# Conditioning columns in the gates stage: partition sums moved one call behind the sums over k, with two buffers between them

## The chip, the cores and the metric

The kernel runs on one core of a Trainium2 chip. The metric is the device time of one execution in microseconds (us); a kernel's time is the median of several executions.

## What is computed

A trunk of two layers works on 1024 latent tokens and 256 context tokens of width 1024. Cut to what matters here, a layer is:

```python
shift, scale, gate = split(silu(c) @ w_ada[l] + b_ada[l], 3)          # for the latent tokens
shift_c, scale_c, gate_c = split(silu(c_ctx) @ w_ada[l] + b_ada[l], 3) # for the context tokens
h = rms(x) * (1 + scale) + shift
... three mixers on parts of h @ w_in[l], each giving a product y @ w_p ...
ga, gb, gc = split(sigmoid(g), 3)                                     # g: the last 3072 columns of h @ w_in[l]
merged = ga * (ya @ w_pa) + gb * (yb @ w_pb) + gc * (yc @ w_pc)
x = x + gate * (merged @ w_out[l])
```

The conditioning vectors shift, scale and gate are 3072 numbers for each of c and c_ctx. They are a product of a vector of 1024 numbers with a 1024 x 3072 matrix. The kernel keeps them as columns: number n stands in partition n mod 128 of column n div 128 of the tile `adac[l]` (24 columns, two variants v, for c and c_ctx).

## The kernel before

Each layer goes through attention, a Fourier stage, products of the mixers, the stage `gates` and the stage `out_phase`. Matrix products in 32-bit precision are made of three matmuls (`mm3`, lines 237 to 239): each operand is split into a rounded part and a remainder (ScalarE at L212 and VectorE at L213 for weights), and TensorE adds high times high, low times high and high times low.

**The gates stage** (`gates`, L671) builds `merged` in blocks of 128 output channels, j = 0 to 7. For every j and every group of 512 latent tokens there are three branches b. For each, TensorE makes a projection of 24 matmuls for the gate (some were made in earlier stages and are fetched back as `lt`), ScalarE takes its tanh (L734), and VectorE multiplies it with the branch's product (`add`, L681 and L684), which is fetched as `lp` or, for b = 1, made by 12 matmuls for each j into a tile shown as `pt` (`product`). GpSimd sums the branches (L685). In layer 0 the context tokens are a third group.

**The conditioning columns** that later stages need are made inside this stage, 256 of them at a time, by `ada_dve` (L177). Layer 0 has twelve such steps, four for its own gate and eight for the shift and scale of layer 1, each for both variants (nv = 2). Layer 1 has four, for one variant. A step has three parts:

- Two DMAs of 512 KB fetch 1024 rows x 256 columns of `w_ada` into two `araw` tiles (L183).
- VectorE takes the sums over k: for each variant eight instructions (L192 for k = 0, L196 for the rest), each of which multiplies a 128 x 256 piece by the scalar of its partition and adds it into `aacc`.
- TensorE sums over the partitions: four matmuls with a column of ones (two for nv = 1) into the PSUM tile `o` (L200); then two small instructions of VectorE add the bias and write `adac` (L202).

`finish`, which `ada_dve` returns, holds the second and third part. `sums` (L690) is called twice for each j, after the first and the fifth of its six branch additions (i = 0 and i = 4). A call runs `finish` of the step whose DMAs the last call issued, and then issues the DMAs of the next step. So step k (from 0) is loaded in call k + 1 and finished in call k + 2. There are 16 calls in the stage, so the last step of layer 0 is finished at j = 6, i = 0.

**What sets the order.** The tile framework is entered with `schedule_with_timeline_sim=True` (L1127). It writes each engine's instruction stream itself, before the run: an instruction is issued when a timeline that the framework keeps has its inputs ready, and among those that are ready the one that stands earlier in the program goes first. Each engine then works through its stream in that fixed order, and waits on the chip where an input is late. `tc.keep_in_program_order(ins)` (L194) pins one instruction behind the one that was traced last on its engine: here the first sum of variant 0. The sums of variant 1 are not pinned. PSUM tiles in the stage are `mm` (2 buffers, projections of the first group), `s` (3, of the second), `pt` (2) and `o` (1) (L98). All DMAs go through the SyncE queue (SP), in order.

`aacc` is one buffer for each nv, taken when `finish` begins, so the first sum of a step must wait until the matmuls of the step before have read it.

Of the kernel before, what the change touches and what calls it, by code (L numbers as in the profile page):

```python
# [11 lines left out]
F32 = mybir.dt.float32  # L12
# [54 lines left out]
def trunk_kernel(ctx: ExitStack, tc: tile.TileContext, a: dict, out: bass.AP):  # L67
# [17 lines left out]
    def bank(tag):  # L85
        tags = banks["tags"]
        tag = tag if tag in tags else "g"
        return banks["pool"].tile([128, 512], F32, tag, bufs=tags[tag])

    def ta(n=512):  # L90
        t = tp.tile([128, 512], F32, "ta", bufs=2)
        return t[:, :n]

    def tb(n=512):
        t = tp.tile([128, 512], F32, "tb", bufs=2)
        return t[:, :n]
# [80 lines left out]
    def ada_dve(l, jb, nv, pool):  # L177

        raws = []
        for half in range(2):  # L180
            raw = pool.tile([128, 4, 256], F32, "araw", bufs=2)
            src = a["w_ada"][l, half * 512:(half + 1) * 512, jb * 128:jb * 128 + 256]
            nc.sync.dma_start(raw, src.rearrange("(k p) c -> p k c", p=128))  # L183
            raws.append(raw)

        def finish():
            acc = pool.tile([128, nv, 256], F32, f"aacc{nv}")
            for k in range(8):
                for v in range(nv):
                    sc = scol[:, k, v:v + 1]  # L190
                    if k == 0:
                        ins = DVE.tensor_scalar(acc[:, v, :], raws[0][:, 0, :], sc, None, ALU.mult)  # L192
                        if v == 0:
                            tc.keep_in_program_order(ins)  # L194
                    else:
                        DVE.scalar_tensor_tensor(acc[:, v, :], raws[k // 4][:, k % 4, :], sc, acc[:, v, :], ALU.mult, ALU.add)  # L196
            pa = bank("o")
            for i in range(2):
                for v in range(nv):
                    PE.matmul(pa[:, 2 * i + v:2 * i + v + 1], acc[:, v, i * 128:(i + 1) * 128], ones[:, 0:1], start=True, stop=True)  # L200
            for i in range(2):
                DVE.tensor_scalar(adac[l][:, jb + i, 0:nv], pa[:, 2 * i:2 * i + nv], bada[l][:, jb + i:jb + i + 1], None, ALU.add)  # L202

        return finish
# [11 lines left out]
    def w_cm(l, c0):  # L216

        return granule(a["w_in"][l, :, c0:c0 + 128].rearrange("(k p) c -> p k c", p=128), [128, KC, 128])
# [17 lines left out]
    def mm3(o, lh, ll, rh, rl, start, stop):  # L236
        PE.matmul(o, lh, rh, start=start, stop=False)  # L237
        PE.matmul(o, lh, rl, start=False, stop=False)  # L238
        PE.matmul(o, ll, rh, start=False, stop=stop)  # L239

    def proj_cm(o, wg, h, n):

        for k in range(KC):
            mm3(o[:, :n], wg[0][:, k, :], wg[1][:, k, :], h[0][k], h[1][k], k == 0, k == KC - 1)
# [14 lines left out]
    def new_h(g):  # L259

        n = GROUPS[g][1]
        pool = bigs["C" if g == "C" else "L"]
        halves = [[pool.tile([128, KC // 2, n], F32R, f"h{x}{i}{g}") for i in range(2)] for x in "hl"]
        H[g] = [[halves[x][k // 4][:, k % 4, :] for k in range(KC)] for x in range(2)]
        return H[g]

    def split(hi, lo, src):
        ACT.copy(hi, src)  # L268
        DVE.tensor_tensor(lo, src, hi.bitcast(F32), ALU.subtract)  # L269
# [274 lines left out]
    def stored(S, key, n):  # L544
        S[key] = dp.tile([128, n], F32, "d" + "_".join(map(str, key)))
        return S[key]
# [6 lines left out]
    def fetched(st, src, n=512, bufs=4, tag="ld"):  # L553
        t = st.tile([128, 512], F32, tag, bufs=bufs)[:, :n]
        nc.sync.dma_start(t, src)
        return t
# [114 lines left out]
    def gates(l, groups, S, ada, side, yb):  # L671

        mp = Pool(tc, name="mp", bufs=1, side=side)
        zq = Pool(tc, name="zq", bufs=1, side=side)
        lat = [g for g in groups if g != "C"]
        hC = new_h("C") if "C" in groups else None
        todo = []

        def add(m, b, t, n, pp):
            if b == 0:  # L680
                DVE.scalar_tensor_tensor(m, t, 1.0, pp, ALU.add, ALU.mult)  # L681
            else:
                s = tb(n)
                DVE.scalar_tensor_tensor(s, t, 1.0, pp, ALU.add, ALU.mult)  # L684
                POOL.tensor_tensor(m, m, s, ALU.add)  # L685

        def branch(b, j, g):
            return fetched(mp, S["P", b, j, g], GROUPS[g][1], 3, f"lp{b}")

        def sums():  # L690
            if todo:
                todo.pop()()
            if ada:
                todo.append(ada_dve(*ada.pop(0), zq))

        def product(j, g):
            n = GROUPS[g][1]
            pp = bank("pt")
            for kb in range(2):
                c = (j % 2) * 128  # L700
                mm3(pp[:, :n], pg[0][:, kb, c:c + 128], pg[1][:, kb, c:c + 128],
                    yb[g][0][:, kb, :], yb[g][1][:, kb, :], kb == 0, kb == 1)
            return pp[:, :n]

        for j in range(8):
            M = {g: mp.tile([128, GROUPS[g][1]], F32, "m" + g, bufs=2) for g in groups}
            W = {}
            if j % 2 == 0:
                raw = zq.tile([128, 2, 256], F32, "praw")
                nc.sync.dma_start(raw, a["w_pb"][l, :, j * 128:j * 128 + 256].rearrange("(k p) c -> p k c", p=128))  # L710
                pg = [zq.tile([128, 2, 256], F32R, f"p{x}") for x in "hl"]
                split(*pg, raw)
            if hC:
                for b in (0, 2, 1):
                    pp = branch(b, j, "C") if b != 1 else product(j, "C")
                    add(M["C"], b, fetched(mp, S["T", b, j, "C"], CTX, 2, "lt"), CTX, pp)
                ACT.activation(hC[0][j], M["C"], AF.Copy, scale=0.5)
                DVE.scalar_tensor_tensor(hC[1][j], M["C"], 0.5, hC[0][j].bitcast(F32), ALU.mult, ALU.subtract)
            order = [(b, g) for b in (0, 1, 2) for g in lat] if j < 7 else [(b, g) for g in lat for b in (0, 2, 1)]
            pb = {}  # L720
            for i, (b, g) in enumerate(order):
                n = GROUPS[g][1]
                if i == 2:
                    pb = {x: product(j, x) for x in lat}
                pp = branch(b, j, g) if b != 1 else pb.pop(g)
                if ("T", b, j, g) in S:
                    t = fetched(mp, S["T", b, j, g], n, 2, "lt")
                else:
                    if b not in W:
                        W[b] = w_cm(l, C_G + b * D + j * 128)  # L730
                    p = bank("mm" if g == "0" else "s")
                    proj_cm(p, W[b], H[g], n)
                    t = ta(n)
                    ACT.activation(t, p[:, :n], AF.Tanh, scale=0.5)  # L734
                add(M[g], b, t, n, pp)
                if i in (0, 4):
                    sums()
                if (b, g) == order[-1] or (g not in [x for _, x in order[i + 1:]]):
                    nc.sync.dma_start(stored(S, ("M", j, g), n), M[g])
        while todo or ada:  # L740
            sums()
        zq.close()
        mp.close()
# [236 lines left out]
    for l in range(DEPTH):  # L980
# [3 lines left out]
        ada = [(l, j, 1 if last else 2) for j in range(16, 24, 2)]  # L984
# [73 lines left out]
        if not last:  # L1058

            se["pool"] = Pool(tc, name="se", bufs=1, side=A)  # L1060
            bigs["C"] = Pool(tc, name="bigC", bufs=1, side="left")
        gates(l, groups, S, ada, A, yb)
        ybp.close()
        xp = Pool(tc, name="xp", bufs=1, side=A)
# [66 lines left out]
```

## Time and profile before

| | |
|---|---|
| time, median of 3 runs | 1931.78 us (1931.34 to 1932.08) |
| the profiled execution's own time | 1932.49 us |
| its span, first to last instruction | 1930.7 us |
| gates stage of layer 0, about | 710 to 972 us of the span |
| gates stage of layer 1, about | 1611 to 1838 us of the span |

The span leaves 1.8 us of the profiled execution's time outside, and that execution was 0.71 us slower than the median. In the views, PE is TensorE's matmuls, PEld its weight loads, DVE is VectorE, ACT is ScalarE, POOL is GpSimd, and SPq is SyncE's queue of DMA issues. An instruction's name is its output, an arrow and its inputs; the number in brackets behind it is how long its engine had been idle, and what ended that. Ends of matmuls are modelled, so a matmul's start is the better mark. A matmul with 32-bit operands that are not split, as at L200, shows as two records with two weight loads: four matmuls are eight records.

### The profile page before, as it was taken

How to read it: one execution, taken by the hardware profiler on the slowest of the kernel's cores; microseconds unless marked ns; L12 is line 12 of the kernel's file. 1: busy time of each engine (PE TensorE's matmuls, PEld its weight loads, DVE VectorE, ACT ScalarE, POOL GpSimd, SP SyncE). 2: the span in 40 equal slices, each digit the busy share in tenths (PEclk: the TensorE clock that was granted, in tenths of full speed). 3: DMA queues.
4: the chain of work that ended last, by engine and by line, in shares of the span. 5: the costliest groups of instructions: out<-in, count | busy, mean ns of one | idle time of the engine just before them, and what ended most of it. 6: DMA issues, size and time to landing. Idle time of an engine off the chain costs nothing.

```text
span 1930.7 us, 31006 instructions
## 1 busy us (share of the span) xinstructions
PE 1884.7 (98%) x10975; PEld 1636.6 (85%) x10975; DVE 1083.1 (56%) x2175; ACT 796.3 (41%) x2088; POOL 608.5 (32%) x975
## 2 busy tenths in 40 slices
PE   7999999999999999999999999999999999999998
PEld 2989999999988887888878998899888788888887
DVE  4665665466665648766355566666565555622342
ACT  2655565455644421111243446555554443111221
POOL 1563344443231112211124464345423021211122
PEclk9999999999999999999999999999999999999999
DMA  9431122213555677554374421212134558632462
GB/s 334 119 106 46 57 65 61 74 43 112 163 181 157 188 226 230 167 178 147 113 259 153 137 72 53 78 42 82 42 100 133 171 183 276 188 105 86 130 222 100
DMA packets 270611, 259.77 MB, mean 135 GB/s; under 512 B 20793, under 2 KB 213497, under 8 KB 270457
## 3 DMA queue, kind: packets, MB, share of 16 engines
q1 hardware_dynamic: 270456, 257.80, 42.1%
q8 instruction: 86, 1.41, 0.3%
q14 instruction: 69, 0.56, 0.1%
HBM read 196.91 MB, written 60.83 MB: 133 GB/s over the span
## 4 chain that ended last, share of the span: by engine, by line
PE 81%; DMA 8%; DVE 4%; POOL 2%; ACT 2%; issue 2%; SPq 1%; POOLq 0%; DVEq 0%; ACTq 0%
PE mm L237 15%; PE mm L238 15%; PE mm L239 15%; PE s L238 6%; PE s L237 6%; PE s L239 6%; PE pt L399 3%; DMA raw<-in_w_in_dram 2%; PE o L406 2%; PE o L407 2%; PE s L371 2%; PE s L364 1%; PE s L365 1%; DVE wlo L213 1%; DMA lt<-dT_C 1%
## 5 line engine op out<-in xcount | busy, mean ns | idle before, releaser
L213 DVE TENSOR_TENSOR wlo<-raw,whi 128x1024 fp32r<-128x1024 f32 (+2 forms) x210 | 243.1, 1160 | 218.4 <-ACT whi L212 213.4
L212 ACT CAST whi<-raw 128x1024 fp32r<-128x1024 f32 (+2 forms) x210 | 202.7, 967 | 374.1 <-PE s L238 146.2
L237 PE MATMUL mm<-hh,whi 128*128 128x512 f32 x720 | 284.2, 395 | 2.9 <-DVE st L562 2.7
L238 PE MATMUL mm<-hl,whi 128*128 128x512 f32 x720 | 282.8, 393 | 0.0
L239 PE MATMUL mm<-hh,wlo 128*128 128x512 f32 x720 | 282.6, 392 | 0.0
L685 POOL TENSOR_TENSOR m<-m,tb 128x512 f32<-128x512 f32 x64 | 87.1, 1363 | 412.1 <-DVE tb L684 369.3
L237 PE MATMUL mm<-whi,hh 128*128 128x256 f32 (+1 forms) x672 | 206.6, 307 | 2.2 <-ACT st L644 1.1
L239 PE MATMUL mm<-whi,hl 128*128 128x256 f32 (+1 forms) x672 | 204.4, 304 | 0.0
L238 PE MATMUL mm<-wlo,hh 128*128 128x256 f32 (+1 forms) x672 | 204.1, 304 | 0.0
L237 PEld LDWEIGHTS mm<-hh,whi 128*128 128x128 f32 x720 | 135.8, 189 | 30.4 <-DVE st L562 3.9
L239 PEld LDWEIGHTS mm<-hh,wlo 128*128 128x128 f32 x720 | 135.6, 188 | 27.1
L238 PEld LDWEIGHTS mm<-hl,whi 128*128 128x128 f32 x720 | 135.8, 189 | 25.9
L238 PE MATMUL s<-hl,whi 128*128 128x512 f32 (+1 forms) x384 | 146.8, 382 | 0.0
L237 PE MATMUL s<-hh,whi 128*128 128x512 f32 (+1 forms) x384 | 146.7, 382 | 0.0
L239 PE MATMUL s<-hh,wlo 128*128 128x512 f32 (+1 forms) x384 | 146.4, 381 | 0.0
L387 POOL TENSOR_SCALAR P<-P,rd 128x640 f32<-128x640 f32 (+2 forms) x144 | 112.8, 794 | 104.1 <-DVE rd L385 68.4
L237 PEld LDWEIGHTS mm<-whi,hh 128*128 128x128 f32 x672 | 127.9, 190 | 8.1 <-ACT st L644 1.6
L238 PEld LDWEIGHTS mm<-wlo,hh 128*128 128x128 f32 x672 | 128.0, 190 | 5.0
L239 PEld LDWEIGHTS mm<-whi,hl 128*128 128x128 f32 x672 | 127.9, 190 | 4.8
L269 DVE TENSOR_TENSOR pl<-pt,ph 128x512 fp32r<-128x512 f32 (+1 forms) x184 | 112.0, 614 | 34.1 <-ACT ph L268 31.6
L268 ACT CAST ph<-pt 128x512 fp32r<-128x512 f32 (+1 forms) x184 | 95.8, 534 | 37.2 <-PE o L406 21.9
L196 DVE SCALAR_TENSOR_TENSOR aacc<-araw,scol,aacc 128x256 f32<-128x256 f32 x196 | 102.1, 554 | 5.8 <-DMA araw<-in_w_ada_dram 3.4
(315 smaller groups left out, 4501.3 us busy)
## 6 DMA issues: line engine op xcount, KB each, us to landing
raw<-in_w_in_dram SPq DMA_DIRECT2D x122, 512.0 KB, 4.1
araw<-in_w_ada_dram SPq DMA_DIRECT2D x48, 512.0 KB, 6.1
raw<-in_w_out_dram SPq DMA_DIRECT2D x40, 512.0 KB, 3.7
dP<-st SPq DMA_DIRECT2D x64, 256.0 KB, 2.4
lp<-dP SPq DMA_DIRECT2D x64, 256.0 KB, 4.3
x<-in_x_dram SPq DMA_DIRECT2D x16, 512.0 KB, 8.2
raw<-in_w_pc_dram SPq DMA_DIRECT2D x32, 256.0 KB, 2.9
dM<-m SPq DMA_DIRECT2D x32, 256.0 KB, 3.4
```

Of the source, the lines that this page charges most:

```text
L196: DVE.scalar_tensor_tensor(acc[:, v, :], raws[k // 4][:, k % 4, :], sc, acc[:, v, :], ALU.mult, ALU.add)
L212: ACT.copy(hi, raw)
L213: DVE.tensor_tensor(lo, raw, hi.bitcast(F32), ALU.subtract)
L237: PE.matmul(o, lh, rh, start=start, stop=False)
L238: PE.matmul(o, lh, rl, start=False, stop=False)
L239: PE.matmul(o, ll, rh, start=False, stop=stop)
L268: ACT.copy(hi, src)
L269: DVE.tensor_tensor(lo, src, hi.bitcast(F32), ALU.subtract)
L371: PE.matmul(bc[:, h * 256:h * 256 + 256], qt[:, s, 2 * pr + h, :], kk[:, g, SEQ:NTOK], start=(h + s == 0), stop=(s == 1), skip_group_check ...
L387: POOL.tensor_scalar(P[hh][:, :nl + 256], P[hh][:, :nl + 256], rd[:, hh:hh + 1], 1.0, ALU.mult, ALU.mult)
L399: PE.transpose(b[:, (2 * i + hh) * 128:(2 * i + hh + 1) * 128], P[hh][:, (i0 + i) * 128:(i0 + i + 1) * 128], ident)
L685: POOL.tensor_tensor(m, m, s, ALU.add)
```

## The change

The partition sums and the writing of `adac` become a function of their own, `columns`, which `finish` returns in place of running it. `sums` keeps it for one call and runs it first thing in the next call, ahead of the next step's sums over k. So step k is loaded in call k + 1, summed over k in call k + 2, and its matmuls and `adac` stand in call k + 3. `acc` is taken when the step's DMAs are issued, and it has two buffers.

```diff
+        acc = pool.tile([128, nv, 256], F32, f"aacc{nv}", bufs=2)
+
         def finish():
-            acc = pool.tile([128, nv, 256], F32, f"aacc{nv}")
             for k in range(8):
                 for v in range(nv):
                     sc = scol[:, k, v:v + 1]
...
                         DVE.scalar_tensor_tensor(acc[:, v, :], raws[k // 4][:, k % 4, :], sc, acc[:, v, :], ALU.mult, ALU.add)
+            return columns
+
+        def columns():
             pa = bank("o")
...
-        todo = []
+        todo, done = [], []
...
         def sums():
+            if done:
+                done.pop()()
             if todo:
-                todo.pop()()
+                done.append(todo.pop()())
             if ada:
                 todo.append(ada_dve(*ada.pop(0), zq))
...
-        while todo or ada:
+        while todo or ada or done:
             sums()
```

## The prediction

> **What bounds the kernel now.** I read the page's head first, then a table of the gates stage in stretches, then the waits of TensorE, and last the moved lines by source and by timeline.
>
> ```profile
> span 1930.7 us, 31006 instructions
> ...
> PE 1884.7 (98%) x10975; PEld 1636.6 (85%) x10975; DVE 1083.1 (56%) x2175; ACT 796.3 (41%) x2088; POOL 608.5 (32%) x975
> ...
> PEclk9999999999999999999999999999999999999999
> ```
> ```profile
> 676.00:730.00 54.00, 53.35 (x253) 44.35 (x252) 24.65 (x38) 14.16 (x23) 7.59 (x7) 1.00 0.72 229
> 730.00:760.00 30.00, 27.60 (x129) 22.21 (x128) 25.21 (x48) 6.23 (x10) 9.43 (x9) 1.00 0.80 246
> 760.00:970.00 210.00, 210.00 (x976) 175.03 (x976) 130.82 (x257) 42.83 (x65) 37.23 (x33) 1.00 0.52 157
> ```
>
> TensorE is busy for 1884.7 of 1930.7 us, so only its idle 46 us can be won by a change that removes no matmul, and this one removes none. The second table has, after the length of each stretch, the busy time of PE, PEld, DVE, ACT and POOL, the granted clock and the DMA share. In layer 0's gates stage, TensorE is idle for 2.40 us between 730 and 760 (30 less 27.60) and never between 760 and 970. There it always has another matmul to go on with, and VectorE is busy for only 130.82 of 210 us. The stage ends when TensorE's work ends.
>
> What the moved lines cost now is in the waits of TensorE and in the view of line 200:
>
> ```profile
> PE o L200 <- DVE aacc L196: 2.8, 3, 1.2
> ```
> ```profile
> L200 PE MATMUL o<-ones,aacc x112: 163/250/272, 736.4 to 1678.4; 128*128 128x1 f32 x112
> ...
>   DVE adac L202: 18.9, 11
> ```
>
> In the whole run TensorE's matmul row waited three times for the sums over k, 2.8 us in all. VectorE in turn waited 11 times, 18.9 us, for these matmuls before writing `adac`. The first number is the prize on the engine that bounds; the second lies on an engine with time to spare.
>
> **The three stops.** In TensorE's timeline they are these:
>
> ```profile
> 734.51 0.39 PE L239 MATMUL s<-hh,wlo 128*128 128x512 f32 x1
> 734.74 0.39 PE L237 MATMUL s<-hh,whi 128*128 128x512 f32 x1
> 736.35 1.05 PE L200 MATMUL o<-ones,aacc 128*128 128x1 f32 x8 [1.23 <-DVE aacc L196]
> 737.27 0.48 PE L237 MATMUL pt<-ybh,ph 128*128 128x512 f32 x1
> ```
> ```profile
> 752.69 0.39 PE L239 MATMUL s<-hh,wlo 128*128 128x512 f32 x1
> 753.87 1.13 PE L200 MATMUL o<-ones,aacc 128*128 128x1 f32 x8 [0.79 <-DVE aacc L196]
> 754.86 0.48 PE L237 MATMUL s<-hh,whi 128*128 128x512 f32 x1
> ```
> ```profile
> 1643.54 0.61 PE L200 MATMUL o<-ones,aacc 128*128 128x1 f32 x4 [0.76 <-DVE aacc L196]
> ```
>
> ```profile
> 809.30 1.06 PE L200 MATMUL o<-ones,aacc 128*128 128x1 f32 x8
> ```
>
> The first three are steps 0 and 1 of layer 0 and step 0 of layer 1: 1.23 + 0.79 + 0.76 = 2.78 us. The other 13 groups, such as step 5's at 809.30, start without a stop. TensorE's stream has the group at a place where the framework expected the sums to be ready, and the chip's VectorE was later than that.
>
> **The change part by part.**
>
> *Matmuls moved.* Sixteen groups of four or two matmuls keep their number and their tiles. One takes 0.92 to 0.99 us from its start to the next matmul's (737.27 less 736.35, 754.86 less 753.87), wherever it stands. Cost: 0.
>
> *Does the move take away the stops?* It lets TensorE put the group later, behind matmuls that now stand ahead of it in the program. That helps only where TensorE, at the moment of the stop, still has such matmuls to do. I counted projections (24 matmuls) and `pt` products (6 for a group of tokens, 12 for a j) along TensorE's timeline. At 736.35 the next matmul is a `pt` product of j = 1, which stands at i = 2 of j = 1; the new place of step 0's group is call 3, at i = 0 of j = 1. TensorE is already past it. At 753.87 TensorE is in the last projection of j = 1 (b = 2, second group, i = 5); the new place of step 1's group is call 4, at i = 4. Past it too. At 1643.54 it is in j = 2; the new place is call 3, at j = 1. Past it again. A group whose place in the program has been passed is issued, as now, when the framework holds its inputs for ready. So the three stops are left standing by the move itself: 0 of 2.78 us. Only later, from about step 5 on, do I find TensorE still short of the new place (its call 8 is at j = 3, i = 4; the group starts at 809.30 now, one projection short of that); those groups will be issued some projections later, and they have no stop to lose.
>
> *The second buffer.* It adds no instruction. It frees the unpinned sums of variant 1 from waiting for the matmuls of the step before. In VectorE's and SyncE's timelines, at step 1:
>
> ```profile
> 737.99 1.04 DVE L718 SCALAR_TENSOR_TENSOR hl0C<-mC,hh0C 128x256 fp32r<-128x256 f32 x1 [0.76 <-ACT hh0C L717]
> 739.86 0.42 DVE L681 SCALAR_TENSOR_TENSOR mC<-lt,lp 128x256 f32<-128x256 f32 x1 [0.82 <-DMA lt<-dT_C]
> 740.20 0.34 DVE L202 TENSOR_SCALAR adac<-o,bada 128x2 f32<-128x2 f32 x2
> 740.46 0.61 DVE L192 TENSOR_SCALAR aacc<-araw,scol 128x256 f32<-128x256 f32 x2
> ```
> ```profile
> 732.13 0.43 SPq L183 DMA_DIRECT2D araw<-in_w_ada_dram  x1
> ```
> ```profile
> DMA to landing us min/median/max: 3.4/4.1/6.8
> ```
>
> The first half of step 1's data was issued at 732.13 and lands between 3.4 and 6.8 us later, by 738.9. VectorE idles 0.82 us just before 739.86, then writes `adac` at 740.20, and only then starts step 1's sums. With its own buffer, one or two sums of variant 1 fit into that 0.82 us. Step 1's sums then end up to 0.8 us sooner, which is what the second stop lasts (0.79). Bounds: 0 if the framework does not use the gap, 0.79 if it does. I take 0.79, since the sums are ready there and nothing else is.
>
> *The pin.* The first sum of variant 0 is now pinned behind the `adac` of the step before, because `columns` runs first in the call. So the pinned half of step k + 1 still follows the matmuls of step k, as it does now through the single buffer. With nv = 1 (layer 1) all sums are pinned. I put this at 0; what it costs if VectorE's cover is gone is the slower rival. A DVE wait holds up the additions and the weight remainders (L213) queued behind it, and through them ScalarE's tanh and TensorE's banks. Waits of this kind already occur where TensorE does not stop:
>
> ```profile
> 781.98 0.35 DVE L202 TENSOR_SCALAR adac<-o,bada 128x2 f32<-128x2 f32 x2 [3.25 <-PE o L200]
> ...
> 918.66 0.34 DVE L202 TENSOR_SCALAR adac<-o,bada 128x2 f32<-128x2 f32 x2 [3.52 <-PE o L200]
> ```
>
> *DMAs.* The `araw` loads of a step are freed by the sums of the step before, not by its matmuls, so SyncE's queue keeps its order and its waits: 0. The last columns come half a j later, at j = 6, i = 4, and their readers stand in the output stage.
>
> *GpSimd.* Sums that start elsewhere meet other additions of GpSimd:
>
> ```profile
> L196 DVE SCALAR_TENSOR_TENSOR aacc<-araw,scol,aacc x196: 471/481/1515, 681.7 to 1674.1; 128x256 f32<-128x256 f32 x196
> ```
> ```profile
> 740.00:840.00 100.00, 98.83 (x464) 81.89 (x463) 79.62 (x166) 18.44 (x27) 20.16 (x17) 1.00 0.61 185
> ```
>
> A sum takes 0.481 us and at worst 1.515, so one can be held for 1.03 us. VectorE has 20.4 us free between 740 and 840, its fullest stretch, and GpSimd runs 17 instructions there; even a new hold by each, 17.5 us, would stay in the free time. I take 0; laid on the stops, a hold would count, and that is rival 5. The Trainium skill, page "SBUF — State Buffer", section "Who interferes with whom", speaks against the change here: it says that a VectorE instruction with two SBUF inputs and a GpSimd instruction that reads SBUF block each other for a whole instruction, the one that started first winning. The trace's longest sums agree with it; by that rule alone, with no free time to hide in, the 17.5 us would be lost in full.
>
> **The sum.** 1932.49 less 0.79 is 1931.7 us for an execution like the profiled one. That execution was 0.71 us above the median of 1931.78, so against the median the forecast is 1931.0 us. From 0 to all 2.78 us won it is 1931.8 to 1929.0.
>
> **The rivals.** What a measurement of this kernel can tell from no change is about 0.2%, 3.9 us.
>
> 1. *All three stops go* because the redrawn streams happen to put other matmuls there: 1931.78 less 2.78 = 1929.0. For it: it is what more distance between sums and matmuls should do. Against it: the counting above. Within 0.2%.
>
> 2. *The change does nothing.* The second buffer goes unused at step 1, the pin keeps the rest in step: 1931.8. For it: the pin. Against it: the idle 0.82 us.
>
> 3. *The redrawn order reaches further.* The framework writes all later streams from its timeline, so a shift in the gates moves ready times behind it, and the many short waits of layer 1's attention and products fall otherwise. Those stages of the two layers show how much waiting there is:
>
> ```profile
> 100.00:660.00 560.00, 549.41 (x3812) 507.86 (x3813) 337.23 (x776) 294.63 (x907) 210.53 (x398) 1.00 0.34 103
> 1120.00:1640.00 520.00, 509.81 (x3157) 450.67 (x3157) 315.77 (x694) 263.28 (x776) 178.30 (x324) 1.00 0.36 114
> ```
>
> TensorE is idle for 10.2 us in the second. If half of that goes, 5.1 us, the time is 1931.0 less 5.1 = 1925.9; if half as much again comes, 1936.1. For it: nothing pins those streams. Against it: most of the new order follows the same priorities.
>
> 4. *Slower: VectorE waits at `adac` for a whole projection.* TensorE does a group at its new place only after the projections that now stand ahead of it, 24 matmuls each, by the 0.23 us from 734.51 to 734.74 an estimated 5.5 us. If VectorE's stream has `adac` earlier than that, VectorE waits up to 5.5 us with additions and remainders behind it. Waits of 3.52 us are covered, as shown; it decides where a wait is longer than that. Price where VectorE is fullest, 740 to 840, with five steps: 5 x (5.5 less 3.5) = 10 us on top of 1931.8, so 1941.8 us. Against it: VectorE's 20.4 free us there.
>
> 5. *Sums held by GpSimd at the stops.* The same 1.03 us, not lost in free time but laid on the three stops that TensorE waits out: 3 x 1.03 = 3.1 us on 1931.78, so 1934.9 us, and still within 0.2%. For it: two sums that are not pinned move at step 1, where GpSimd's additions run. Against it: the other two stops have their sums where they were.
>
> **How the numbers follow.** Forecast (second stop gone, 1931.0): 0.37. Rival 1: 0.12. Rival 2: 0.09. Rival 5: 0.04. Rival 3: faster by more than 0.2% 0.22, slower by as much 0.09. Rival 4: 0.07. The first four are within 0.2%: 0.62. Faster 0.22, slower 0.09 + 0.07 = 0.16. The range takes rival 3 on both sides, 1925.9 to 1936.1, and leaves out rival 4 and what lies beyond; the forecast with rivals 1 and 2 alone spans 1929.0 to 1931.8.
>
> **What would show it.** Right: in the new profile the waits of L200 for L196 stay above 1 us in total, with the first stop near 736 still there; from step 5 on the groups stand after a completed projection and no longer inside one; VectorE's 18.9 us before `adac` shrink; TensorE stays at 210 of 210 us between 760 and 970. Wrong: those waits at zero (rival 1), or TensorE idle by some us behind 740 with VectorE waiting over 3.5 us at `adac` (rival 4), or a difference over 3.9 us that arises outside the gates (rival 3).

## The result, and the profile after

The change made the kernel slower. Its median is 1948.02 us (1947.49 to 1951.42) against 1931.78 us (1931.34 to 1932.08), a ratio of 1.0087 with a 95% interval of 1.0074 to 1.0100. (The ratios of this document come from all runs of both kernels; they are not the quotients of the two medians and differ from them by up to 0.001.) The profiled execution took 1947.56 us, 15.1 us more than the profiled one of before. The head of the page of after:

```profile
span 1945.8 us, 30995 instructions
...
PE 1889.7 (97%) x10975; PEld 1638.9 (84%) x10975; DVE 1091.9 (56%) x2175; ACT 797.2 (41%) x2088; POOL 610.3 (31%) x975
```

TensorE does the same 10975 matmul records and its busy time is 5.0 us longer; the other 10 us are idle time. The table of stretches of after shows where (columns as in the prediction: busy time of PE, PEld, DVE, ACT and POOL, granted clock, DMA share, GB/s):

```profile
730.00:760.00 30.00, 26.43 (x118) 21.33 (x118) 24.76 (x46) 5.75 (x9) 8.96 (x8) 0.94 0.78 242
760.00:820.00 60.00, 50.72 (x216) 40.78 (x216) 42.99 (x85) 7.74 (x12) 7.13 (x6) 0.91 0.60 136
820.00:970.00 150.00, 150.00 (x699) 125.01 (x698) 86.30 (x160) 26.56 (x40) 29.03 (x25) 1.00 0.45 142
```

TensorE is idle for 3.57 us between 730 and 760 and for 9.28 us between 760 and 820, together 12.85 us where before had 2.40. That is 10.45 us. The granted clock, 1.00 in both stretches before, is 0.94 and 0.91. From 820 on TensorE is busy throughout again, as before. The first partition sums start at 734.36 in after and at 736.35 in before, 2.0 us earlier; the last ones, in layer 1, start at 1693.4 and 1678.4, 15.0 us later. So the whole loss is made in the first 90 us of layer 0's gates, where it is about 17 us; the 2.0 us come from the stages ahead of it, where nothing was changed. TensorE's and VectorE's waits of after between 700 and 990 (engine, what it did, what it waited for: us in total, times, longest) name the causes:

```profile
PE pt L241 <- DVE tb L688: 6.2, 1, 6.2
PE o L204 <- DVE aacc L197: 4.3, 4, 1.3
PE pt L243 <- DVE pl L273: 2.4, 1, 2.4
```
```profile
DVE aacc L193 <- DMA araw<-in_w_ada_dram: 23.2, 11, 9.9
...
DVE aacc L197 <- DMA araw<-in_w_ada_dram: 6.3, 3, 3.2
```

The same two rows of VectorE in the view of before, with the one that stood at the top there:

```profile
DVE mC L681 <- DMA lt<-dT_C: 19.2, 7, 6.7
...
DVE adac L202 <- PE o L200: 14.4, 9, 3.5
...
DVE aacc L196 <- DMA araw<-in_w_ada_dram: 1.3, 2, 1.0
```

VectorE used to wait 1.3 us for the loads of `w_ada` and now waits 23.2 + 6.3 = 29.5 us. The two longer stops of TensorE are for VectorE's other work, a `tb` and a weight remainder, which stand behind such waits in VectorE's stream. Of these, the 2.4 us at 746.41 are only in part the change's. In before TensorE waited 0.38 us for the same remainder, and VectorE began it at 744.80 there and at 744.61 here; TensorE merely came to it two us earlier in after. The longest stop can be followed through three timelines of after. SyncE's, with the landing of the loads issued there:

```profile
788.98 1.05 SPq L910 DMA_DIRECT2D gate<-adac  x2
790.13 0.97 SPq L745 DMA_DIRECT2D dM<-m  x1
791.67 2.46 SPq L183 DMA_DIRECT2D araw<-in_w_ada_dram  x2
```
```profile
DMA to landing us min/median/max: 12.0/12.0/12.0
```

VectorE's:

```profile
788.73 1.35 DVE L193 TENSOR_SCALAR aacc<-araw,scol 128x256 f32<-128x256 f32 x1
790.12 3.61 DVE L197 SCALAR_TENSOR_TENSOR aacc<-araw,scol,aacc 128x256 f32<-128x256 f32 x7
803.66 0.35 DVE L193 TENSOR_SCALAR aacc<-araw,scol 128x256 f32<-128x256 f32 x1 [9.94 <-DMA araw<-in_w_ada_dram]
803.93 1.22 DVE L217 TENSOR_TENSOR wlo<-raw,whi 128x1024 fp32r<-128x1024 f32 x1
...
809.18 0.41 DVE L688 SCALAR_TENSOR_TENSOR tb<-lt,pt 128x256 f32<-128x256 f32 x1
```

TensorE's:

```profile
803.07 0.40 PE L243 MATMUL pt<-ybh,pl 128*128 128x512 f32 x1
809.65 0.79 PE L241 MATMUL pt<-ybh,ph 128*128 128x512 f32 x1 [6.18 <-DVE tb L688]
810.24 0.63 PE L242 MATMUL pt<-ybl,ph 128*128 128x512 f32 x1
810.67 0.63 PE L243 MATMUL pt<-ybh,pl 128*128 128x512 f32 x1
```

VectorE ends one step's sums at 793.7, and the next instruction of its stream is the first sum of the next step. That step's load could be issued only when these sums set the `araw` tiles free, at 791.67, and it took 12.0 us to land where loads had taken 3.4 to 6.8. VectorE stands for 9.94 us with weight remainders, more sums and the additions behind it. At 809.18 it reads the `pt` tile whose bank TensorE needs, and TensorE has been idle for 6.18 us.

After the stop the matmuls start 0.43 us apart (810.24, 810.67) where they had taken 0.23. There are 13 such until about 815.4, and 8 each after the stops at 746.41 and 793.87, so (13 + 8 + 8) x 0.20 = 5.8 us. With the 10.45 us of idle time that is 16.2 us, against the 15.1 by which the two profiled executions differ and the 17 above; in before single matmuls behind the partition sums took 0.31 to 0.33 us (about 0.6 us in these 90).

Why the load took 12.0 us is in the table of after around it, and in the DMA view of after between 788 and 800:

```profile
792.00:796.00 4.00, 2.87 (x15) 2.18 (x14) 1.62 (x4) 0.60 (x1) 0.00 (x0) 0.87 0.91 17
796.00:800.00 4.00, 4.00 (x14) 3.21 (x13) 0.00 (x0) 0.00 (x0) 0.00 (x0) 0.71 0.90 40
```
```profile
DMA packets 2436, 0.61 MB, mean 50 GB/s; under 512 B 2106, under 2 KB 2183, under 8 KB 2436
```

The DMA engines are 0.9 busy and move only 17 and 40 GB/s, in small packets. Ahead of the load in SyncE's queue, with one store of 256 KB between, stand two DMAs that the prediction passed over: `gate<-adac` (L910), the gate columns of step 3 written out as a row in HBM, one for each v. They are part of the output stage, but the columns are complete with step 3, so the framework issues them at once. Each is 4 KB in 1024 pieces of 4 bytes, together 2048 of the small packets above. Before had them too; its SyncE timeline:

```profile
782.36 0.99 SPq L904 DMA_DIRECT2D gate<-adac  x2
```

Behind them stood a weight, a load of `w_ada` and a fetched `lt`. The DMA view of the weight's issue:

```profile
raw<-in_w_in_dram SPq DMA_DIRECT2D x1, 512.0 KB, 11.8
```

The weight took 11.8 us to land and the `lt` 12.5, and VectorE waited the 6.7 us above, for the `lt`. TensorE did not feel that. The DMA engines were only 0.1 to 0.4 busy there between 783 and 795, so their being busy is not what the two cases share; how the two DMAs hold up what follows is not shown.

### The profile page after: what moved, and what is told of

Its sections match the earlier page's. It is cut to its first block, busy times and chain, and to the rows that moved or that the text cites. A ratio compares the mean times of both kernels' runs of the same rounds, so it can differ in the third digit from the quotient of the medians.

```text
span 1945.8 us, 30995 instructions
## 1 busy us (share of the span) xinstructions
PE 1889.7 (97%) x10975; PEld 1638.9 (84%) x10975; DVE 1091.9 (56%) x2175; ACT 797.2 (41%) x2088; POOL 610.3 (31%) x975
## 4 chain that ended last, share of the span: by engine, by line
PE 80%; DMA 9%; DVE 5%; ACT 2%; issue 2%; POOL 1%; SPq 1%; POOLq 0%; DVEq 0%; ACTq 0%
PE mm L241 15%; PE mm L242 15%; PE mm L243 15%; PE s L241 7%; PE s L242 7%; PE s L243 6%; PE pt L403 3%; DMA araw<-in_w_ada_dram 3%; DMA raw<-in_w_in_dram 2%; PE o L410 2%; PE o L411 2%; PE s L375 1%; PE s L368 1%; DVE aacc L197 1%; PE s L369 1%
## 5 line engine op out<-in xcount | busy, mean ns | idle before, releaser
L197 DVE SCALAR_TENSOR_TENSOR aacc<-araw,scol,aacc 128x256 f32<-128x256 f32 x196 | 108.0, 554 | 12.5 <-DMA araw<-in_w_ada_dram 7.6
```

## The experiments

Two theories came out of this. **Early sums:** the second buffer lets the unpinned sums of variant 1 stand right behind the sums of the step before, ahead of their load, and all of VectorE's stream waits with them. **Collision:** the two `gate<-adac` DMAs hold up what comes behind them, and it matters only what that is. Their rival is the move itself: matmuls and `adac` one call later. Each kernel below is compared with the kernel before on the same chip; those medians were 1931.55 (first four), 1932.24 (next four) and 1933.30 us (last four).

**The move alone.** One buffer, taken in `finish` as before; the columns one call behind.

```diff
+            return columns
+
+        def columns():
...
+            if done:
+                done.pop()()
             if todo:
-                todo.pop()()
+                done.append(todo.pop()())
```

> The move without the second buffer: the partition sums stand one call behind the sums over k, but the accumulator is one buffer again, taken when the sums over k begin. Theory (early sums): the loss comes from the sums of variant 1, which are not pinned and which the second buffer sets free to be issued straight behind the sums of the step before; their data land later on the chip, and VectorE stands in front of them with additions queued behind. Without the buffer they wait for the matmuls as before, so 1929 to 1934 us and VectorE waits for the loaded columns for under 5 us in layer 0's gates. Rival (the move itself): matmuls and adac at their later place hold VectorE and TensorE up; then about 1948 us.

Measured: 1933.86 us, ratio 1.0007 (0.9995 to 1.0019). Waits of VectorE in the gates, between 700 and 990:

```profile
DVE mC L685 <- DMA lt<-dT_C: 10.6, 6, 6.7
```

There is no row for `araw`. The move costs nothing and gains nothing that can be measured; the collision falls on a fetched `lt`, as before, and costs nothing either.

**The buffers alone.** The matmuls where they were; two buffers, taken when the loads are issued.

```diff
+        acc = pool.tile([128, nv, 256], F32, f"aacc{nv}", bufs=2)
+
         def finish():
-            acc = pool.tile([128, nv, 256], F32, f"aacc{nv}")
```

> The kernel before with two accumulator buffers taken when the loads are issued, and the partition sums in their old place. Early sums: the buffer alone sets variant 1 free, so about 1944 to 1950 us, with more than 15 us of VectorE waiting for the loaded columns. The move itself: 1931 to 1933 us.

Measured: 1944.39 us, ratio 1.0072 (1.0054 to 1.0091). Waits of VectorE between 700 and 990:

```profile
DVE aacc L193 <- DMA araw<-in_w_ada_dram: 18.5, 9, 8.4
DVE aacc L197 <- DMA araw<-in_w_ada_dram: 4.6, 3, 1.7
```

The second buffer by itself brings the waits for loads and most of the loss. The longest wait, 8.4 us, is for a load that took 10.4 us to land, behind the same two DMAs.

**The change with both first sums pinned.**

```diff
-                        if v == 0:
-                            tc.keep_in_program_order(ins)
+                        tc.keep_in_program_order(ins)
```

> The changed kernel, with the first sum of variant 1 pinned in program order as that of variant 0 is. Early sums: the early issue is gone and with it the stops, 1928 to 1934 us. The move itself: still about 1948 us.

Measured: 1942.11 us, ratio 1.0054 (1.0035 to 1.0073). The waits for `araw` are gone but for 1.7 us. In their place stand these, in the timelines of VectorE and of TensorE:

```profile
799.37 0.43 DVE L684 SCALAR_TENSOR_TENSOR mC<-lt,lp 128x256 f32<-128x256 f32 x1 [8.69 <-DMA lt<-dT_C]
```
```profile
803.65 1.84 PE L203 MATMUL o<-ones,aacc 128*128 128x1 f32 x8 [5.64 <-DVE aacc L196]
```

In this kernel the gate DMAs are issued at 785.37 and 789.01, with two `lt` fetches between them, and VectorE waits 8.69 us for an `lt`, 2.0 us longer than before. TensorE stops for 5.64 us at the partition sums, whose sums over k stand behind that wait. Early sums alone as the cause falls here: without them the kernel is still slower, with the collision in another place.

**The change with the gate DMAs kept in the output stage.**

```diff
-            nc.sync.dma_start(row.rearrange("j p -> p j"), adac[l][:, 16:24, v])
+            tc.keep_in_program_order(nc.sync.dma_start(row.rearrange("j p -> p j"), adac[l][:, 16:24, v]))
```

> The changed kernel, with the DMAs that write the gate columns as rows pinned in program order on SyncE's queue, so that they are issued in the output stage and no longer at about 789 us, in front of a load of w_ada that then takes 12 us to land. Early sums with this collision as a part of it: the stop of 6.2 us near 804 shrinks to about 1 us and the slow matmuls behind it go, so 1939 to 1943 us; the other stops stay. If the collision is the whole cause: 1931 to 1934 us. If it has no part: 1948 us.

Measured: 1948.08 us, ratio 1.0092 (1.0069 to 1.0115), no better. The tables of this kernel and then of after, gates and output stage:

```profile
760.00:840.00 80.00, 76.66 (x361) 63.29 (x360) 65.93 (x129) 13.76 (x21) 15.04 (x12) 1.00 0.54 169
970.00:1090.00 120.00, 111.96 (x504) 90.89 (x503) 68.05 (x79) 49.51 (x68) 40.21 (x38) 0.97 0.58 195
```
```profile
760.00:840.00 80.00, 70.72 (x310) 57.58 (x310) 55.69 (x108) 11.52 (x17) 11.01 (x9) 0.94 0.57 139
970.00:1090.00 120.00, 118.62 (x545) 97.40 (x543) 70.22 (x81) 51.38 (x71) 40.50 (x39) 1.00 0.57 194
```

In the gates TensorE does 361 matmuls in the 80 us in place of 310, and the 6.18 us stop is gone, so it does not arise without the collision. But the output stage loses 118.62 less 111.96 = 6.7 us again; its longest wait is 5.3 us for a weight's high part of ScalarE. The gate DMAs now stand just ahead of that stage, at 945.41 and 956.58. The second took 13.7 us to land, and the DMA that reads the row back waited for it and held SyncE's queue for 8.9 us, until 970.30. That this wait makes the loss of the output stage is likely, but no run shows it. The total, which stayed at 1948, could not show the gain.

**The change with the gate DMAs late in the gates** (j = 6, i = 5), where no load of `w_ada` follows them.

```diff
+                if (j, i) == (6, 5):
+                    for v in range(1 if l == DEPTH - 1 else 2):
+                        S["gate", v] = dp.tile([KC, 128], F32, f"gate{l}{v}")
+                        tc.keep_in_program_order(nc.sync.dma_start(S["gate", v].rearrange("j p -> p j"), adac[l][:, 16:24, v]))
...
-            row = dp.tile([KC, 128], F32, f"gate{l}{v}")
-            nc.sync.dma_start(row.rearrange("j p -> p j"), adac[l][:, 16:24, v])
+            row = S["gate", v]
```

> The changed kernel, with the DMAs that write the gate columns as rows issued at j = 6, i = 5 of the gates stage, pinned in SyncE's order: neither at 789 us in front of a load of w_ada nor in front of the output stage's loads. Two causes (early sums, and this collision): the stops of 0.7 to 2.5 us that come from early sums stay, the stop of 6.2 us goes, and nothing is lost in the output stage, so 1936 to 1941 us. Early sums alone: 1946 to 1950 us. Collision alone: 1929 to 1934 us.

Measured: 1939.50 us, ratio 1.0030 (1.0016 to 1.0045). Waits of VectorE between 700 and 990:

```profile
DVE aacc L193 <- DMA araw<-in_w_ada_dram: 15.2, 11, 3.0
DVE mC L685 <- DMA lt<-dT_C: 10.1, 4, 8.1
DVE aacc L197 <- DMA araw<-in_w_ada_dram: 5.8, 3, 3.5
```

Of the loss, 1.0087 less 1.0030, about two thirds, go with the collision. The other third stays with the early sums: there are as many waits for `araw` as in after (11 and 3), only none over 3.5 us.

**Both mended:** the late gate DMAs and both pins.

> The changed kernel with both mendings: the first sums of both variants pinned, and the gate rows written at j = 6, i = 5. Two causes: both are gone, 1929 to 1934 us. If something else in the change costs time (the move or the pin behind adac): 1938 us or more, with TensorE stops in layer 0's gates that name neither a load of w_ada nor a late lt.

Measured: 1931.42 us, ratio 1.0006 (0.9992 to 1.0020). The loss is gone, and nothing is gained on before. One row of VectorE's timeline is worth keeping:

```profile
918.36 0.42 DVE L684 SCALAR_TENSOR_TENSOR mC<-lt,lp 128x256 f32<-128x256 f32 x1 [10.03 <-DMA lt<-dT_C]
```

The collision is still there, now behind j = 6, and VectorE waits 10.03 us for an `lt`. TensorE has no wait at all between 840 and 990.

**Before with the late gate DMAs**, as the control for the last two.

> The kernel before, with the gate rows written at j = 6, i = 5. Two causes: in the kernel before the collision falls on a fetched gate tile and VectorE waits 6.7 us for it, which TensorE does not feel; so 1930 to 1933 us, no change. If the collision costs TensorE time there too: 1925 to 1928 us.

Measured: 1940.64 us, ratio 1.0038 (1.0024 to 1.0052), which no theory expected. In the timelines of VectorE and TensorE:

```profile
918.06 0.43 DVE L681 SCALAR_TENSOR_TENSOR mC<-lt,lp 128x256 f32<-128x256 f32 x1 [8.85 <-DMA lt<-dT_C]
```
```profile
925.64 1.84 PE L200 MATMUL o<-ones,aacc 128*128 128x1 f32 x8 [3.97 <-DVE aacc L196]
```

The same collision at the same place, with a shorter wait than with both mended, stops TensorE for 3.97 us here, at the partition sums that still stand close behind the sums over k. This speaks for the move: it buys distance between sums and matmuls; only, in the kernel as it was, nothing used it up. It is not isolated, since the two kernels also differ in the second buffer and in the second pin.

**The late gate DMAs without the loads.** The change with the late gate DMAs and no further pin; `w_ada` is loaded only for the first step of each layer, and all steps use that data.

```diff
+            if len(kept[-1]) == 2:
+                raws = kept[-1]
+                break
             raw = pool.tile([128, 4, 256], F32, "araw", bufs=2)
...
+            kept[-1].append(raw)
```

> The changed kernel with the gate rows at j = 6, i = 5, and w_ada loaded only for the first step of each layer; every later step sums the same data again, so the loads of the other steps are left out and the columns are not the reference's. Early sums: nothing is late in front of VectorE, its waits for loaded columns go below 2 us and TensorE's stops in the gates below 4 us, 1927 to 1933 us. If VectorE's order itself (not the late data) costs: as the run with the gate rows alone, 1936 to 1941 us.

Measured: 1931.73 us, ratio 0.9991 (0.9979 to 1.0004). VectorE has no wait for `araw`. The early sums themselves are harmless; their waits for the loads are the third that was left. (The loads' traffic is gone as well, so this run alone would not prove it; the pins show it with all traffic in place.)

**The gate rows in large pieces.** Is it the place of the gate DMAs or their 4-byte pieces? Here they stand at j = 3, i = 2 of the program, near the place that after has, but TensorE transposes the columns first and the row is written in pieces of 512 bytes.

```diff
+                if (j, i) == (3, 2):
+                    for v in range(1 if l == DEPTH - 1 else 2):
+                        pr, rw = bank("o"), tb(128)
+                        PE.transpose(pr[0:8, 0:128], adac[l][:, 16:24, v], ident)
+                        DVE.tensor_copy(rw[0:8, :], pr[0:8, 0:128])
+                        S["gate", v] = dp.tile([KC, 128], F32, f"gate{l}{v}")
+                        nc.sync.dma_start(S["gate", v], rw[0:8, :])
...
-            row = dp.tile([KC, 128], F32, f"gate{l}{v}")
-            nc.sync.dma_start(row.rearrange("j p -> p j"), adac[l][:, 16:24, v])
+            row = S["gate", v]
```

> The changed kernel, where the gate columns are turned into rows by two small TensorE transposes at j = 3, i = 2 and written as runs of 512 bytes, in place of 1024 pieces of 4 bytes for each variant. Two causes: the small pieces are what held the load of w_ada for 12 us, so without them that stop is gone and the early sums' stops stay, 1936 to 1941 us, and no load of w_ada takes over 8 us to land. If the place and not the pieces was the trouble: 1944 to 1950 us.

Measured for the change with these rows: 1941.08 us, ratio 1.0038 (1.0026 to 1.0051), about the same as with the late DMAs. The transposes run at 810.77 and 818.42, so the rows leave only at 818.40 and not at about 789. Their issue and the next one in SyncE's timeline, with the DMA view of the latter:

```profile
818.40 1.77 SPq L750 DMA_DIRECT2D gate<-tb  x2
821.01 0.40 SPq L213 DMA_DIRECT2D raw<-in_w_in_dram  x1
```
```profile
raw<-in_w_in_dram SPq DMA_DIRECT2D x1, 512.0 KB, 3.8
```

The weight behind these rows takes 3.8 us to land, where in before the one behind the 4-byte pieces took 11.8; no load of `w_ada` in the gates takes over 6.5. The 4-byte pieces held up what followed at every place where they were issued: near 785, at 903 to 910 and at 957. So the pieces are the trouble. Place matters only through what stands behind them; 4-byte pieces at 818 were not tried. The other three kernels of this kind:

> The same rows by transposes in the changed kernel with the first sums of both variants pinned: neither cause is left. 1928 to 1932 us, so no slower than the kernel before, and VectorE's longest wait for a fetched tile in the gates under 7 us. If something in the change itself costs: 1936 us or more.

Large pieces and both pins: 1932.64 us, ratio 1.0002 (0.9991 to 1.0013). The second way of mending both causes ends at the same place as the first; here a load of `w_ada` stands directly behind the first row, and VectorE waits for no load of `w_ada` at all.

> The same rows by transposes in the kernel before: its collision, which made VectorE wait 6.7 us for a fetched gate tile, is gone, and TensorE never felt it: 1929 to 1933 us, no difference. If it cost TensorE time: 1925 to 1928 us.

Before with large pieces: 1933.81 us, ratio 1.0008 (0.9997 to 1.0019). VectorE's longest wait for an `lt` falls from 6.7 to 3.4 us, for no gain in time. So before paid nothing for the collision.

> The same rows by transposes with the partition sums one call behind and one buffer. Two causes: none of them is here, so 1928 to 1932 us, as with rows and both pins; a gap of more than 4 us between these two would show that the second buffer still costs something when its early sums are pinned.

The move alone with large pieces: 1934.80 us, ratio 1.0013 (1.0001 to 1.0025). That is above the expected range, and 2.2 us above the kernel with rows and both pins, so the second buffer costs nothing that shows here once its sums are pinned. Here too nothing is won. No kernel of the twelve beats before by more than its interval.

## Why the prediction was wrong

*The bound* was read rightly: TensorE bounds the stage, and the loss is its idle and half-rate time, in the stage that the prediction treated. That TensorE "always has another matmul to go on with" there held for before only: in after it is busy for 50.72 of the 60 us from 760 to 820.

*The move* went as worked out. The first stop stands where it was, and from step 5 on the groups stand behind a completed projection, as these rows of TensorE's timeline of after show:

```profile
734.36 1.05 PE L204 MATMUL o<-ones,aacc 128*128 128x1 f32 x8 [1.19 <-DVE aacc L197]
```
```profile
829.95 0.39 PE L243 MATMUL mm<-hh,wlo 128*128 128x512 f32 x1
830.17 0.95 PE L204 MATMUL o<-ones,aacc 128*128 128x1 f32 x8
830.98 0.49 PE L241 MATMUL s<-hh,whi 128*128 128x512 f32 x1
```

Alone it measured 1.0007, within the "0 of 2.78 us" and what can be told from no change. VectorE's wait before `adac` shrank from 18.9 us to 5.3 in the whole run of after.

*The second buffer* is the step that failed. It was bounded by "0 if the framework does not use the gap, 0.79 if it does", a gain or nothing. The prediction asked what the freed sums no longer wait for, the matmuls of the step before, and looked at one step only, where the first half of the load had already landed. It did not ask what they wait for next. In before, the single buffer kept them behind the matmuls and so gave the load time to land; once that wait goes, the load is what ends last, and it can be issued only when the sums of the step before set its tiles free. The framework's own timeline is not on record; that the loads came sooner in it than on the chip is inferred from the order that it drew. Its price was 1.0072 with the buffers alone, a collision included, and 1.0030 to 1.0038, some 6 to 7 us, where the collision was taken out of the change.

*DMAs* failed with it: "SyncE's queue keeps its order and its waits: 0". The gate row's DMAs were not looked at. What stood behind them could be late without harm; now the load that VectorE's stream waits for stands behind them.

*Rival 4* had the right shape, a long wait of VectorE with additions and remainders behind it, and the right sign. It had the wrong wait: not `adac` for a projection, but the sums for their load. Its limit of 3.52 us was too low. VectorE's wait of 6.66 us in before is survived between 740 and 840, and those of 8.4 us (buffers alone), 8.69 and 9.94 are not; at 918, 8.85 us costs TensorE 3.97 us with the matmuls near and 10.03 us costs nothing with them one call later.

*GpSimd* was put at 0. The first sums grew; the two rows are before's and after's groups by line between 660 and 1060:

```profile
L192 DVE TENSOR_SCALAR aacc<-araw,scol 128x256 f32<-128x256 f32 x24 | 8.4, 366 | 0.4 <-DMA araw<-in_w_ada_dram 0.3
```
```profile
L193 DVE TENSOR_SCALAR aacc<-araw,scol 128x256 f32<-128x256 f32 x24 | 14.7, 611 | 23.8 <-DMA araw<-in_w_ada_dram 23.8
```

That is 6.3 us more of VectorE, next to which it stood idle for 29.5 us. It was not isolated by a run. The prediction took 740 to 840 for VectorE's fullest stretch; 730 to 760 was fuller, 25.21 of 30 us.

*Still open:* why `lt` took 8.69 us with both pins where before had 6.66, and how much of the loss the fall of the clock would make by itself.

## What to carry to other kernels

Before you free an instruction of an in-order engine from a wait, ask which of its inputs is then the last to come, and what is queued behind that wait; a second buffer that a scheduler may use freely is also a licence to place work too early. Look at the neighbours in the DMA queue of each load that becomes urgent: a transfer of 4 KB in 4-byte pieces took up to 13.7 us to land here, and a load of 512 KB of `w_ada` that was not behind it 3.4 to 6.8. If such a transfer costs nothing now, it does so only because what stands behind it may be late.

## What the runs showed of the hardware

After two DMAs of 4 KB in 4-byte pieces, in after, the DMA engines were 0.9 busy for some 8 us at 17 to 40 GB/s, and a load of 512 KB behind them took 12.0 us to land. In before a load of 512 KB behind them took 11.8 us, with the engines 0.1 to 0.4 busy up to 795. Behind the same rows in 512-byte pieces such a load took 3.8 us.

The clock fell after short stops. TensorE's timeline of after:

```profile
793.87 1.02 PE L204 MATMUL o<-ones,aacc 128*128 128x1 f32 x8 [1.13 <-DVE aacc L197]
794.76 0.62 PE L241 MATMUL s<-hh,whi 128*128 128x512 f32 x1
795.17 0.63 PE L242 MATMUL s<-hl,whi 128*128 128x512 f32 x1
795.60 0.63 PE L243 MATMUL s<-hh,wlo 128*128 128x512 f32 x1
```

After a stop of 1.13 us and 0.89 us of one-column matmuls, the matmuls start 0.43 us apart, and the granted clock between 796 and 800 is 0.71. After the stop of 1.23 us in before, with 0.92 us of such matmuls behind it, the matmuls start 0.23 us apart from the second on. The Trainium skill, page "TensorE: Matmul & The Clock Gate", section "What's actually happening", lets the clock halve after at least one idle window of about 3.4 us, and says that the window runs freely. The factor agrees (0.43 for 0.23); the length does not, since stop and one-column matmuls together are 2.0 us here. What tells the two stops apart was not tried.
